# A fourth staging tile, an earlier place for one input tile and a later copy of turned keys in a one-core hybrid layer

## The chip, the core and the metric

The kernel runs on one core of a Trainium2 chip. The metric is the time of one execution on the device in microseconds (us), and the median of three runs is compared. TensorE (PE in the profile) multiplies matrices, VectorE (DVE), ScalarE (ACT) and GpSimd (POOL) work on elements, and SyncE (SP) issues nearly all transfers between device memory and on-chip memory. Each engine takes its instructions in the order in which the program lists them, so an instruction that waits holds up everything listed behind it on the same engine.

## The reference

One layer of a streaming encoder is computed for 2048 new rows (the prompt) and for 64 rows that continue an older stream (the sample), each row with 1024 features:

```
h = h + concat[ attnA(xn) * silu(gA), hgrn2(xn) * silu(gB) ] @ W_out,   xn = RMSNorm(h)
[aq, ak, av, ag, hq, hf, hi, hg] = split(xn @ W_in)        # eight groups of 512 columns
attnA: 8 heads x 64, chunks of 64 rows, each sees itself and the 8 chunks before it, plus a learned bias
hgrn2: 4 heads x 128, f = lb + (1-lb) sigmoid(hf), S_t = diag(f_t) S_{t-1} + (1-f_t) i_t^T, o_t = S_t^T q_t
y = RMSNorm(h)
```

Besides y, the new keys and values and the recurrent states are returned. Products are made in single precision's reduced form with operands split into a high and a low part, so each projection runs three passes (high by high, low by high, high by low).

## The kernel before

**Tiles and stages.** The rows are worked off in four super-blocks (`SUPER`): 512 rows, 512 rows and the 64 sample rows, 512, 512. In each there are 32 jobs: one job projects all rows of the super-block on 128 columns of W_in (24 matmuls for each piece of up to 512 rows, `project`, line 539). The jobs go by heads of the recurrence (`hf`, `hq`, `hi`, `hg`) and pairs of attention heads (`pg`, `pq`, `pk`, `pv`). A job's product lies in one of two PSUM banks named `acc`. It is taken out of there by an evacuation (`ev_q`, `ev_k`, `ev_v`, `ev_i` and others). These four kinds put it into a staging tile named `vT` of 128 x 512 numbers, of which there are three (`VTB`, line 31). `ev_v` and `ev_i` turn the tile by 32 x 32 blocks on VectorE and then send it through device memory and back (`turn_rows`, line 697: four transfers `way<-vT`, one transfer `vT<-way`), and the tile stays taken until the values are copied out. When the jobs are done, the output stage multiplies with W_out (by seven products for every 256 rows), adds the residual rows and normalizes.

**What sets the order.** The program is a planner that lists instructions for all engines by hand. `Plan` (line 52) holds a clock `now`, which goes on with each matmul listed, and for each other engine the time when it will be free by estimated costs (`act`, `dve`, `pool`, `dma`: a transfer is priced at 2.8 ns for each KB on SP plus 3500 ns). The main program lists the projections. Beside it run threads: evacuations, attention, recurrence, loads. A thread says what it waits for: a time, an engine's queue that will be at most 800 ns behind (`("D", t)`), a condition, or a token (`Tok`) that stands for a buffer. `pump` goes through the threads by rank, lower numbers first, and lists what is ready. Evacuations have rank 0, attention and recurrence 1, weights 2. The real chip then runs these fixed lists. Real waits come from semaphores, so where the estimate was too short an engine stands still.

**Input tiles.** `x_tile` (line 351) brings in 128 rows of the input (64 for the sample): it takes one of three `xn` buffers, loads it (line 358), squares it on ScalarE (line 368), makes 1/rms (lines 336 and 337), scales it on VectorE (line 382), waits until the older super-block has no more use of that half of `xh` and `xl` (line 387), and transposes it on TensorE by way of PSUM (line 397). `x_split` (line 404) copies the high part (409) and subtracts it for the low part (415). Only when the last transposes of a tile are listed is its `xn` buffer given back (line 401). The five tiles of super-block 1 are spawned together eight jobs before the end of super-block 0 (line 2104): rows 0 and 128 with rank 0.5, rows 256, 384 and 512 (the last is the sample's tile) with rank 0.6. The second half of super-block 1 needs the tiles 256, 384 and 512.

**Turned keys.** In super-blocks after the first the recurrence of the heads 0 and 1 turns its keys `kh` in the same way through device memory (line 1497, tiles `bl` and `way`). Line 1531 waits in the plan until the estimated time `rows["t"]` of the return. Then ScalarE copies the turned keys (line 1534) and TensorE multiplies them with the values (line 1560). The PSUM bank `g` and the token `rec` are held meanwhile.

**Output stage.** `residual` (line 1672) gives a residual tile one of four rooms. The fourth, named by the token `x5`, consists of a tile `rest` and a tile `sga`. `rest` and the token come in `out_rows_g` (line 2145). `out_load` takes two `vT` tiles for the inputs of every second 256 rows and a third for a sum.

Of the kernel before, what the change touches and what calls it, by code (L numbers as in the profile page):

```python
# [8 lines left out]
F32 = mybir.dt.float32  # L9
# [8 lines left out]
P = 128  # L18
# [9 lines left out]
RAWB = 2  # L28
XNB = 3
PRB = 4  # L30
VTB = 3
BIG = 1e30
NEVER = 1e30
QUEUE = 800.0
# [149 lines left out]
def hymba_step(  # L184
# [34 lines left out]
    wk = ctx.enter_context(tc.tile_pool(name="wk", bufs=2))  # L219
# [3 lines left out]
    C = Plan()  # L223
    uid = [0]

    def T(pool_, shape, dt, tag, **kw):
        uid[0] += 1
        return pool_.tile(list(shape), dt, tag=tag, name=f"{tag}_{uid[0]}", **kw)
# [122 lines left out]
    def x_tile(sb, half, c, here=None, gain=None):  # L351

        off, bn = SUPER[sb][3][half]
        rows = min(P, off + bn - c)
        if here is None:
            yield from tk["xn"].get()
            xn = T(px, [P, D], F32, "xn", bufs=XNB)
            sp.dma_start(xn[:rows], x_rows(sb, c, rows))
            t = C.dma(512)
        else:  # L360
            xn, t = here
        if half and not sb:
            yield lambda: x_there.get((0, 0, 0), (0, 0))[0] == 4
        yield "A", t
        yield from tk["ck"].get()
        junk = T(wk, [P, D], mybir.dt.bfloat16, "ck", bufs=1)
        ss = T(wk, [P, 1], F32, "ss", bufs=4)
        act.activation(junk[:rows], xn[:rows], AF.Square, accum_out=ss[:rows])
        r = rstd_of(ss, rows, D)
        tk["ck"].put()  # L370
        t = C.act(1700, t)
        have.add(f"r{c // P}")
        if not sb:
            yield lambda: "gain" in have and (not half or x_there.get((0, 0, 1), (0, 0))[0] == 4)
        g = g_in[:rows]
        cut = (slice(0, 512), slice(512, D)) if not sb else (slice(0, D),)
        ends = []
        for k0 in (0, 4):
            if k0 == 0 or not sb:
                c_ = cut[k0 // 4]  # L380
                yield "D", t
                dve.scalar_tensor_tensor(xn[:rows, c_], xn[:rows, c_], r[:rows], gain[k0 // 4] if gain else g[:, c_],
                                         ALU.mult, ALU.mult)
                t = C.dve(c_.stop - c_.start + 20, t)
                if k0:
                    have.add(f"s{c // P}")
            yield lambda: x_left.get((sb - 1, half), False)
            yield t
            tags = ("g", "tr") if sb else ("tr", "pv", "g") if half else ("tr", "pv", "acc")
            while not any(tk[x].n for x in tags):  # L390
                some = [tk[x].when() for x in tags]
                yield min(some) if min(some) < NEVER else C.now + 150.0
            tag = [x for x in tags if tk[x].n][0]
            tk[tag].take()
            pt = psum(tag, bufs={"g": 1, "pv": 1}.get(tag, 2))
            for kt in range(k0, k0 + 4):
                transpose(pt[:, (kt - k0) * P : (kt - k0) * P + rows], xn[:rows, kt * P : (kt + 1) * P],
                          ident[:rows, :rows])
            ends.append((k0, tag, pt, C.pe()))
            if k0 and here is None:  # L400
                tk["xn"].put(1, C.pe())
            C.spawn(x_split(sb, half, c, rows, *ends[-1]), 0 if sb or half else -1)
# [970 lines left out]
    def rec_block(r, off, bn, lastb):  # L1373
# [154 lines left out]
        if by_dma:  # L1528
            yield ta + 200.0
            yield lambda: "t" in rows  # L1530
            yield rows["t"]
            kn = tmp("k1").rearrange("p (c t) -> p c t", t=P)
            if nprc:
                act.copy(kn[:, :nprc].rearrange("p c (a j) -> p c a j", j=32),
                         kh[:, :full].rearrange("p (a c j) -> p c a j", a=4, j=32))
            if bn > full:
                act.copy(kn[:DEC, nprc], kh[:DEC, full : full + P])
                pool.memset(kn[DEC:, nprc], 0.0)
            t = C.act(bn, rows["t"])
            yield t + 200.0  # L1540
        else:
            yield max(ta, tkh) + 200.0
            tg = bank()
            for i, (cc, nbk, smp) in enumerate(chunks):
                w = nbk * 32
                transpose(tg[:w, i], kh[:, cc : cc + w], ident)
            t = C.pe()
            yield "A", t
            kn = tmp("k1").rearrange("p (c t) -> p c t", t=P)
            for cs, w in merged():  # L1550
                act.copy(kn[:w, cs], tg[:w, cs])
                if w < P:
                    pool.memset(kn[w:, cs], 0.0)
            t = C.act(bn, t)
            yield t + 200.0
# [110 lines left out]
    more = []  # L1666
# [352 lines left out]
    def program():  # L2019
# [66 lines left out]
        for sb in range(nsb):  # L2086
            last = sb == nsb - 1
            halves = SUPER[sb][3]
            blocks = SUPER[sb][2]
            if sb == 2:  # L2090
                C.spawn(out_weights(), 3)
            made = {}
            for u, (kind, g) in enumerate(JOBS[sb]):
                if u == len(JOBS[sb]) - 8:
                    if last:
                        C.spawn(out_load(0), 1.5)
                        C.spawn(out_load(1), 1.6)
                        for rows in (out_rows_w(), out_rows_g(), out_rows_x(), out_rows_a()):
                            C.spawn(rows, 2)
                    else:  # L2100
                        for half in range(2):
                            off, bn = SUPER[sb + 1][3][half]
                            for c in range(off, off + bn, P):
                                C.spawn(x_tile(sb + 1, half, c), 0.5 + 0.1 * half)
                if (kind[0], g) not in made:
                    d, evs = made[kind[0], g] = (head_jobs if kind[0] == "h" else pair_jobs)(sb, g)
                    C.spawn((recurrence if kind[0] == "h" else attention)(d), 1)
                evac = made[kind[0], g][1][kind[1]]

                if u == 1 or (u == len(JOBS[sb]) - 1 and not last):  # L2110
                    for half in range(2):
                        yield from project(j - 1, [halves[half]], before, half == 1,
                                           lambda part, k0: x_ready(sb, half, part, k0))
                        yield from project(j, [halves[half]], evac, half == 1,
                                           lambda part, k0: x_ready(sb, half, part, k0))
                        if u > 1:
                            x_left[sb, half] = True
                elif u != 0 and (last or u != len(JOBS[sb]) - 2):
                    yield from project(j, blocks, evac)
                    if u == len(JOBS[sb]) - 1:  # L2120
                        x_left[sb, 0] = x_left[sb, 1] = True
                before = evac
                j += 1
# [3 lines left out]
    def wo_load(k, w):  # L2127

        for part in range(2):
            hi = w(part, None)  # L2130
            for r, c in hi:
                sp.dma_start(f32(r), wod[k][:, part, c])
        wo[k] = (lambda part, kt: w(part, kt), C.dma(2048))

    def flat4(hi, lo):
        def w(part, kt):
            x = (hi, lo)[part]
            if kt is None:
                return [(x.rearrange("p (k n) -> p k n", k=4), slice(0, 4))]
            return x[:, kt * 512 : kt * 512 + 512]  # L2140

        return w


    def out_rows_g():
        yield lambda: done_g.get((len(SUPER) - 1, 3), 0) >= WIN
        yield C.now + 5000.0
        stkG.close()
        pw = ctx.enter_context(tc.tile_pool(name="pw", bufs=1, side="right"))
        turns = [0]  # L2150

        def slot():


            turns[0] += 1
            if turns[0] % 5 == 0:
                c = slice(8 * 512, 9 * 512)
                return [x.rearrange("p k n -> p (k n)")[:, c].rearrange("p (k t) -> p k t", t=P) for x in (xh, xl)]
            m = T(pw, [P, 2, 4, P], F32R, "slot", bufs=4)
            return m[:, 0], m[:, 1]  # L2160

        more.append(lambda: T(pw, [P, 512], F32, "rest"))
        tk["x5"].put()
        C.spawn(out_parts(slot), 1)
        wo_load(0, flat4(*(T(pw, [P, 4 * 512], F32R, f"b11{x}") for x in "hl")))

    def out_rows_w():
        yield lambda: len(order) - 1 in w_at
# [103 lines left out]
```

## Time and profile before

| what | value |
|---|---|
| median of three runs | 1229.98 us |
| lowest and highest run | 1228.17 and 1233.73 us |
| the profiled execution | 1236.85 us |
| its span, first to last instruction | 1234.9 us |
| TensorE busy | 1213.7 us, 98% of the span |
| VectorE, ScalarE, GpSimd busy | 897.7, 678.9, 416.2 us |
| mean granted TensorE clock | 0.995 |
| moved by DMA | 294.42 MB, 238 GB/s over the span |

A row of a timeline has start, duration, engine and line, operation, output<-input, shape and count, and in brackets the idle time of that engine just before and who ended it. A row of the waits has the total idle time in us, how often, and the longest. A row of the windows gives for a stretch of time its length, the busy time and number of instructions of PE, PEld (weight loads), DVE, ACT and POOL, then the granted TensorE clock as a share of the full clock, the DMA share and GB/s.

### The profile page before, as it was taken

Reading aid. Unit: us, or ns where it says so; the run is one execution under the profiler, and the core shown is the slowest. Engines: PE = TensorE matmul, PEld = TensorE weight load, DVE = VectorE, ACT = ScalarE, POOL = GpSimd, SP = SyncE. Lnnn points to the kernel's source line nnn. Section 1 sums busy time; section 2 is a strip of 40 time slices with the busy share of each in tenths; the row PEclk is TensorE's granted clock in tenths of the full one; section 3 lists DMA queues with packets and bytes.
Section 4 is the critical chain, followed back from the end, with each engine's and each line's share of the span. In section 5 each row is a group of like instructions: output and inputs, shape, how many; then the busy total and the mean of one; then the engine's idle time right before and its main releaser. Section 6 shows DMA issues by size and latency. Waiting matters only on the chain.

```text
span 1234.9 us, 22287 instructions
## 1 busy us (share of the span) xinstructions
PE 1213.7 (98%) x7914; PEld 1069.1 (87%) x7914; DVE 897.7 (73%) x1897; ACT 678.9 (55%) x1526; POOL 416.2 (34%) x715
## 2 busy tenths in 40 slices
PE   9999999899999999999999999999989999999997
PEld 8888888899999999998888888988778888888786
DVE  6697879766867687686587768775747665967775
ACT  6354546655565557574556566665636545644443
POOL 7665564111120110200232241133332203575543
PEclk9999999999999999999999999999989999999999
DMA  8898888657475585565887788587968586987431
GB/s 340 305 325 291 292 299 326 210 167 246 158 231 157 153 273 182 192 210 177 290 267 230 274 294 285 195 277 243 282 214 263 187 289 210 356 275 239 131 134 68
DMA packets 158328, 294.42 MB, mean 238 GB/s; under 512 B 51657, under 2 KB 98377, under 8 KB 140554
## 3 DMA queue, kind: packets, MB, share of 16 engines
q1 hardware_dynamic: 157784, 292.74, 71.0%
q8 instruction: 62, 1.02, 0.3%
q14 instruction: 48, 0.39, 0.1%
q10 hardware_dynamic: 434, 0.27, 0.1%
HBM read 198.52 MB, written 95.49 MB: 238 GB/s over the span
## 4 chain that ended last, share of the span: by engine, by line
PE 85%; DMA 9%; ACT 2%; DVE 1%; SPq 1%; issue 1%; POOL 0%; ACTq 0%; POOLq 0%; DVEq 0%
PE acc L249 56%; PE pv L249 7%; PE g L249 7%; PE tr L253 5%; PE s L249 5%; PE tr L249 4%; DMA vT<-way 1%; DMA bl<-way 1%; PE g L1369 1%; DMA w<-wd 1%; DMA ck<-in_cache_attn_v_dram 1%; DMA way<-vT 1%; DMA mixd<-ob 1%; DMA bias<-biasd 1%; DMA carry<-kd 1%
## 5 line engine op out<-in xcount | busy, mean ns | idle before, releaser
L249 PE MATMUL acc<-xh,w 128*128 128x512 f32 (+2 forms) x2720 | 563.5, 347 | 0.5 <-ACT vT L816 0.5
L249 PEld LDWEIGHTS acc<-xh,w 128*128 128x128 f32 x2720 | 437.1, 190 | 50.8 <-ACT vT L816 0.8
L249 PE MATMUL acc<-xl,w 128*128 128x512 f32 (+2 forms) x1360 | 293.8, 348 | 0.0
L249 PEld LDWEIGHTS acc<-xl,w 128*128 128x128 f32 x1360 | 223.3, 191 | 25.6
L967 ACT ACTIVATE pr<-pr,nm 128x640 f32<-128x640 f32 (+4 forms) x132 | 100.4, 761 | 61.2 <-DVE nm L950 60.2
L950 DVE CUSTOM_DVE_ANT_0 pr<-s,bias 128x640 f32<-128x640 f32 (+4 forms) x128 | 94.2, 736 | 48.2 <-PE s L249 45.6
L979 ACT CAST ph<-tr 128x512 fp32r<-128x512 f32 (+3 forms) x176 | 87.1, 507 | 75.3 <-PE tr L253 36.4
L982 DVE TENSOR_TENSOR ph<-tr,ph 128x512 fp32r<-128x512 f32 (+3 forms) x176 | 101.2, 589 | 28.3 <-ACT ph L979 27.3
L473 POOL TENSOR_TENSOR w<-wraw,w 128x256 fp32r<-128x256 f32 x120 | 101.6, 875 | 58.2 <-DVE w L468 33.4
L249 PE MATMUL pv<-ph,v 128*128 128x256 f32 (+2 forms) x344 | 97.1, 370 | 2.2 <-DVE ph L982 1.6
L253 PE MATMUL tr<-ident,pr 128*128 128x128 f32 x580 | 87.3, 273 | 0.9 <-DVE ph L982 0.9
L510 POOL TENSOR_TENSOR xn<-wraw,xn 128x256 fp32r<-128x256 f32 x48 | 39.8, 831 | 143.5 <-ACT xn L507 142.1
L1021 DVE TENSOR_TENSOR mixa<-mixa,pv 64x256 f32<-64x256 f32 (+1 forms) x144 | 56.8, 394 | 38.9 <-ACT mixa L1017 35.4
L1611 POOL TENSOR_TENSOR k<-ob 128x512 f32<-128x512 f32 (+2 forms) x20 | 18.4, 920 | 192.8 <-ACT ob L1602 192.5
L971 DVE TENSOR_SCALAR pr<-pr,sm 128x640 f32<-128x640 f32 (+4 forms) x132 | 79.8, 604 | 4.7
L253 PEld LDWEIGHTS tr<-ident,pr 128*128 128x128 f32 x580 | 69.7, 140 | 10.0 <-DVE ph L982 1.3
L1123 POOL TENSOR_TENSOR mixa<-mixa,sga 128x256 f32<-128x256 f32 (+1 forms) x36 | 28.7, 797 | 140.6 <-DVE mixa L1021 87.0
L249 PEld LDWEIGHTS pv<-ph,v 128*128 128x128 f32 x344 | 59.2, 190 | 10.4 <-issue 1.4
L575 ACT ACTIVATE sig<-acc 128x512 f32<-128x512 f32 (+2 forms) x63 | 31.9, 507 | 64.1 <-PE acc L249 63.0
L1017 ACT COPY mixa<-pv 64x256 f32<-64x256 f32 (+1 forms) x72 | 25.1, 349 | 60.3 <-PE pv L249 54.2
L249 PE MATMUL s<-kd,q 128*128 128x320 f32 (+2 forms) x232 | 55.8, 311 | 0.7 <-DVE nm L950 0.5
L249 PE MATMUL s<-kd,ql 128*128 128x320 f32 (+2 forms) x232 | 55.7, 310 | 0.0
(420 smaller groups left out, 2090.2 us busy)
## 6 DMA issues: line engine op xcount, KB each, us to landing
w<-wd SPq DMA_DIRECT2D x96, 1024.0 KB, 6.1
wd<-w SPq DMA_DIRECT2D x32, 1024.0 KB, 7.7
wraw<-in_w_in_dram SPq DMA_DIRECT2D x30, 512.0 KB, 5.5
wod<-xn SPq DMA_DIRECT2D x28, 512.0 KB, 5.3
xn<-in_x_prompt_dram SPq DMA_DIRECT2D x23, 512.0 KB, 5.3
bias<-biasd SPq DMA_DIRECT2D x24, 320.0 KB, 6.1
carry<-kd SPq DMA_DIRECT2D x12, 512.0 KB, 6.1
carry<-v SPq DMA_DIRECT2D x12, 512.0 KB, 7.2
```

The source lines that it names most:

```text
L249: pe.matmul(out, w, x, **kw)
L253: pe.transpose(out, x, idn)
L473: pool.tensor_sub(w[:, 1, k : k + 2], raw[:, k : k + 2], f32(w[:, 0, k : k + 2]))
L510: pool.tensor_sub(f32r(st[:, c.start + 512 : c.stop + 512]), src[:, c], st[:, c])
L575: act.activation(sig[:, :bn], acc, AF.Exp, scale=-1.0)
L950: dve.tensor_tensor_reduce(s[:, :nk].rearrange("p (a c) -> p a c", a=ns), sps[:, :ns, :kn], d.bias[:, h, bcol : bcol + nk].rearrange("p (a ...
L967: act.activation(s[:, :nk], s[:, :nk], AF.Exp, bias=nm[:, 0:1], scale=-1.0, accum_out=sm)
L971: dve.tensor_scalar(s[:, :nk], s[:, :nk], sm, None, ALU.mult)
L979: act.copy(ph[:krows, 0, :wid], pt[:krows, :wid])
L982: dve.tensor_sub(ph[:krows, 1, :wid], pt[:krows, :wid], f32(ph[:krows, 0, :wid]))
L1021: dve.tensor_add(mix[hs, :qn], mix[hs, :qn], pv[hs, i, :qn])
L1123: pool.tensor_mul(mix[:, :n], mix[:, :n], d.sg[:, g0 : g0 + n])
```

## The change

There are four edits. There are four `vT` tiles and four tokens for them, not three. A load of an input tile is priced by its rows, which for the sample's tile halves the size from 512 to 256. At the super-block's end an input tile of fewer than 128 rows, which is the sample's, is spawned with rank -0.5, ahead of the evacuations' rank 0. In the last super-block the copy of the turned keys is listed 3000 ns later in the plan. In the output stage the tile `rest` goes: the fourth room's first tile is one of the four `vT` tiles, it is taken after all projections of the last super-block are evacuated ("projected"), and only then is the token `x5` given.

```diff
-VTB = 3
+VTB = 4
@@ x_tile
             sp.dma_start(xn[:rows], x_rows(sb, c, rows))
-            t = C.dma(512)
+            t = C.dma(512 * rows / P)
@@ rec_block, if by_dma:
             yield lambda: "t" in rows
-            yield rows["t"]
+            yield rows["t"] + (3000.0 if sb == len(SUPER) - 1 else 0.0)
             kn = tmp("k1").rearrange("p (c t) -> p c t", t=P)
@@ program
                             for c in range(off, off + bn, P):
-                                C.spawn(x_tile(sb + 1, half, c), 0.5 + 0.1 * half)
+                                C.spawn(x_tile(sb + 1, half, c), 0.5 + 0.1 * half if off + bn - c >= P else -0.5)
@@ out_rows_g
-        more.append(lambda: T(pw, [P, 512], F32, "rest"))
-        tk["x5"].put()
         C.spawn(out_parts(slot), 1)
         wo_load(0, flat4(*(T(pw, [P, 4 * 512], F32R, f"b11{x}") for x in "hl")))
+        yield lambda: "projected" in have
+        yield from tk["vT"].get()
+        more.append(lambda: T(wk, [P, 512], F32, "vT", bufs=VTB))
+        tk["x5"].put()
```

## The prediction

> **What bounds the kernel now.** I read the page first, then whom TensorE waits for, then windows and timelines around its two longest waits.
>
> ```profile
> span 1234.9 us, 22287 instructions
> PE 1213.7 (98%) x7914; PEld 1069.1 (87%) x7914; DVE 897.7 (73%) x1897; ACT 678.9 (55%) x1526; POOL 416.2 (34%) x715
> ```
>
> TensorE is busy for 1213.7 of 1234.9 us. No edit takes a matmul away, so only its 21.2 us of idle time can be gained, and what it loses at a lower clock. Its waits:
>
> ```profile
> PE g L249 <- ACT k L1534: 3.8, 2, 3.4
> PE g L253 <- DVE xn L382: 3.3, 1, 3.3
> PE tr L253 <- DVE ph L982: 1.7, 2, 0.9
> PE pv L249 <- DVE ph L982: 1.6, 2, 1.0
> PE pv L2068 <- POOL one L279: 1.4, 1, 1.4
> PE g L249 <- DVE So L1572: 0.7, 2, 0.4
> PE pv L249 <- DVE v L683: 0.6, 1, 0.6
> PE s L249 <- DVE nm L950: 0.5, 1, 0.5
> PE acc L249 <- ACT vT L816: 0.5, 1, 0.5
> ```
>
> Two waits stand out, and two edits aim at them: the turned keys (line 1534) and an input tile (line 382). Without the one at the start (line 2068), the short ones and the 0.4 us left of the first row sum to 6.0 us. There is hardly a sign that staging tiles are short: TensorE waited for an evacuation into `vT` once, for 0.5 us.
>
> Windows around the two waits, and one with two short gaps, show a second cost in the clock column (after the busy times):
>
> ```profile
> 240.00:244.00 4.00, 0.70 (x8) 0.58 (x8) 3.65 (x8) 2.28 (x7) 0.00 (x0) 1.00 0.86 320
> 245.00:249.00 4.00, 4.00 (x18) 3.80 (x17) 3.93 (x17) 3.04 (x12) 2.02 (x9) 0.57 0.17 62
> 904.00:908.00 4.00, 0.97 (x5) 0.46 (x3) 0.00 (x0) 0.29 (x1) 0.00 (x0) 0.95 0.97 347
> 908.00:915.00 7.00, 6.62 (x22) 5.69 (x23) 4.73 (x11) 2.88 (x7) 3.09 (x4) 0.54 0.50 143
> 789.00:796.00 7.00, 5.71 (x44) 5.00 (x43) 6.80 (x14) 5.54 (x13) 1.99 (x2) 1.00 0.76 231
> ```
>
> After each long wait TensorE goes on at about half the clock: 4.00 us at 0.57 lose 4.00 x 0.43 = 1.72 us, 6.62 us at 0.54 lose 6.62 x 0.46 = 3.05 us. The last stretch, with 1.29 us of gaps, stays at 1.00. So the input tile's wait costs 3.30 + 1.72 = 5.02 us, the keys' 3.41 + 3.05 = 6.46 us (hundredths from the timelines below), together 11.48 us.
>
> By the Trainium skill (TensorE: Matmul & The Clock Gate, Part 1), the clock falls to half after an idle window of about 3.4 us and returns after a busy one, the windows running freely: 1.7 us for each wait. The trace agrees at the first (1.72) and has nearly twice that at the second. By the rule's figure in place of 3.05 the forecast below would be 1225.7 us.
>
> **The turned keys, 3000 ns later.** Where the second wait comes from:
>
> ```profile
> 889.58 2.01 PE L249 MATMUL acc<-xl,w 128*128 128x512 f32 x8
> 897.80 1.00 SPq L715 DMA_DIRECT2D bl<-way  x1
> 907.71 0.62 ACT L1534 COPY k<-bl 128x512 f32<-128x512 f32 x1 [6.74 <-DMA bl<-way]
> 908.24 0.36 ACT L979 CAST ph<-tr 128x256 fp32r<-128x256 f32 x1
> 908.38 2.08 PE L249 MATMUL g<-gi,k 128*128 128x128 f32 x8 [3.41 <-ACT k L1534]
> 912.39 2.50 PE L249 MATMUL acc<-xl,w 128*128 128x512 f32 x6
> DMA to landing us min/median/max: 1.4/2.5/9.9
> ```
>
> The way back was issued at 897.80 and landed 9.9 us later, where the median of tile `bl`'s transfers is 2.5. The copy held ScalarE for 6.74 us, and behind it in ScalarE's list stood the copy for `ph` (908.24) and more, on which later matmuls depend. The edit lists the copy, and the matmuls on the keys with it, 3.0 us of planned time later, so that other matmuls pass them. There are such: between 910.0 and 914.7 stand ten of a running projection (the row at 912.39 has six) and two on `ph`, twelve at 2.01 / 8 = 0.25 us at full clock, or 3.0 us, and ScalarE lists the copy for `ph` before the wait then. The wait of 3.41 shrinks to 0.41 us, a gap of the sort after which the clock stayed at 1.00. Gain: 3.0 + 3.05 = 6.05 us. The bounds: 6.46 if the way back is faster in the new order, nothing if it is 3 us slower still. I take 6.05, since the edit leaves the transfer and its neighbours where they are.
>
> Behind the copy on its path are the state updates on VectorE, the store of a state on SP, two more rounds on TensorE, GpSimd's square (line 1611) and the store to `mixd`; all move by the same 3 us, and the bank `g` and `rec` are held as long. The next recurrence has room for that:
>
> ```profile
> 924.03 0.75 DVE L1629 SCALAR_TENSOR_TENSOR ob<-ob,gnorm,k 128x512 f32<-128x512 f32 x1
> 943.61 0.68 DVE L1388 TENSOR_TENSOR bm<-gb 128x512 f32<-128x512 f32 x1
> ```
>
> One ends its norm at 924.8, the next begins at 943.6, so 19 us cover 3; without them the 3 us would be paid in full. Cost taken: nothing.
>
> **The sample's input tile ahead of evacuations.** Here the plan's tokens decide, more than the rank that the edit names:
>
> ```profile
> 174.95 1.40 SPq L358 DMA_DIRECT2D xn<-in_x_prompt_dram  x3
> 225.46 0.33 SPq L358 DMA_DIRECT2D xn<-in_x_prompt_dram  x1
> 227.97 0.57 SPq L358 DMA_DIRECT2D xn<-in_x_sample_dram  x1
> 232.69 1.04 PE L253 MATMUL tr<-ident,xn 128*128 128x128 f32 x8
> 234.29 1.06 ACT L368 ACTIVATE ck<-xn 64x1024 bf16<-64x1024 f32 x1
> 235.80 0.20 ACT L337 ACTIVATE rstd<-rstd 64x1 f32<-64x1 f32 x1
> 238.85 0.29 DVE L683 TENSOR_TENSOR v<-vT,v 128x128 fp32r<-128x128 f32 x1 [0.27 <-ACT v L680]
> 240.00 0.57 ACT L409 CAST xh<-tr 128x512 fp32r<-128x512 f32 x1
> 242.42 1.27 DVE L382 SCALAR_TENSOR_TENSOR xn<-xn,rstd,gin 64x1024 f32<-64x1024 f32 x1
> 243.83 0.43 PE L253 MATMUL g<-ident,xn 64*128 64x64 f32 x4 [3.30 <-DVE xn L382]
> 244.30 0.37 ACT L409 CAST xh<-g 128x256 fp32r<-128x256 f32 x1 [1.95 <-PE g L253]
> ```
>
> Three tiles (rows 0, 128, 256) are loaded near 175, into all three buffers. Tile 384 and the sample's come when the first two give theirs back, at 225.46 and 227.97. The last one's 1/rms was there at 236.00, but VectorE scaled it at 242.42, behind evacuations from 238.85 on, and TensorE, out of other work, waited from 240.53.
>
> With rank -0.5 the sample's thread is first in `pump` also when the tokens are given out. So it takes one of the three buffers near 175, and its load, square, 1/rms and scaling move from 228 to 244 down to 175 to 191, where tile 256 stood. But it can't be transposed there: its half of `xh` is free only at about 232.69, where the edited plan puts it and the old one tile 256. Until then it keeps its buffer, so tile 256 is loaded at about 225.5 and tile 384 at about 228. Tile 384 has rank 0.6 as the sample's tile had. It gets the last place with the same wait behind the evacuations, and with more to do: each of its two high copies takes 0.57 rather than 0.37 us. SP's queue has 512 KB in that place and 256 KB in the earlier one; the transfers behind it are the bias windows and a weight, due later. The price of 256 shortens the plan's SP clock by 0.72 us at 175, where nothing waits.
>
> So the 5.02 us stay and about 2 x 0.20 = 0.4 us are added. The bounds: -5.02 if the tile comes forward after all (VectorE's list from 238.85 to 242.42 is 3.57 us, more than the 3.30), and some +1.5 if the doubled load holds ScalarE. I take +0.4, since the queue that made the wait is unchanged and only the tile in it differs.
>
> **The fourth tile.** It adds no instruction. It lets the plan list an evacuation earlier, so every list after the first shortage is in another order. What the trace shows to be gained is 0.5 us at `acc`; what it can cost is rivals two and three. I take nothing. In the output stage a fourth `vT` tile replaces `rest`:
>
> ```profile
> L1701 SPq DMA_DIRECT2D rest<-in_x_prompt_dram x2: 430/920/1411, 1099.8 to 1137.1; - x2
> ```
>
> That room is first used at 1099.8, and it needs the last scores as it did before, which come after the projections. The later token costs nothing, and the loads are as many.
>
> **The sum.** 6.05 - 0.4 = 5.65 us. The profiled execution took 1236.85 us (1.95 over its span), so 1231.2. It lies above all three runs; the median is 1229.98 / 1236.85 = 0.99445 of it, which makes **1224.4 us**. Its own range is 1221 to 1227. About 0.5% (6.1 us, the line being at 1223.8) is what a measurement of this kernel can tell from no change, and the forecast lies at that line.
>
> **The rivals.**
>
> *One, both long waits go.* The sample's tile still comes last or the new order clears VectorE's list near 240, and no tile is late. For: 3.57 us of evacuations stood before the scaling. Against: the buffers. Gain 5.02 + 6.05 = 11.07, so 1219 us. With the 6.0 us of short waits closed too, 1213.
>
> *Two, a new long wait opens elsewhere.* The two of now cost 5.02 and 6.46, on the mean 5.7. One more eats the gain: 1230 us. For: all lists change, and ScalarE has many places where it waits in line for a round trip:
>
> ```profile
> ACT v L680 <- DMA vT<-way: 16.9, 9, 5.0
> ACT gi L1308 <- DMA vT<-way: 12.0, 10, 3.8
> ```
>
> Against: these 19 waits, of up to 5.0 us, stopped TensorE for no more than 1 us now.
>
> *Three, slower: the round trips crowd.* With four tiles, four trips can be open at once rather than three. If transfers then land later than the plan allows, ScalarE's waits above outlast TensorE's listed work, each time for idle time and half a clock. It decides from the third: 3 x 5.7 - 5.65 = 11.5 us lost, or 1241 us. Against: the number of trips is the same.
>
> *Four, the clock stays down.* The keys' wait shrinks, but the gaps left around it keep the clock low: only 3.0 of the 6.05 are gained, 1227.4 us. The row from 789 to 796 speaks against it. The Trainium skill (TensorE: Matmul & The Clock Gate, "A second HAM failure mode: psum-queue depth-cycling") tells of short idles between matmul groups making the clock go to and fro; in that row the trace disagrees.
>
> *Five, the keys are as late in their new place.* Nothing is gained: 1230.4 us.
>
> **How the numbers follow.** The forecast has 0.36, rival one 0.24 (0.04 of it with the short waits closed), two 0.18, three 0.13, four 0.04, five 0.05. Half of the forecast lies beyond 0.5%: faster 0.18 + 0.24 = 0.42, slower 0.13 and a little of rival two, 0.15, the rest 0.43. The range goes from 1215, between the two ends of rival one, to 1233, which is rival two with the 1.5 us of tile 384 and rounding; it leaves out rival three and the 0.04.
>
> **What would show it.** Right: TensorE's row for line 1534 has under 0.5 us as its longest, and the clock after it is 1.00; a row for line 382 still has 3 to 4 us, now on a tile of 128 rows, with the sample's load near 175 and a prompt load near 228. Wrong: no row for line 382, or new rows of 3 us and more, above all behind `vT<-way`; a busy time of TensorE that differs by more than the clock explains.

## The result and the profile after

| | before | changed |
|---|---|---|
| median of seven runs | 1229.98 us | 1225.01 us |
| ratio, with its 95% interval | | 0.9948 (0.993 to 0.9966) |
| profiled execution | 1236.85 us | 1225.67 us |
| its span | 1234.9 us | 1223.9 us |

One of the seven runs before took 1491.62 us in a slow state of the chip, and the ratios here and below leave such runs out. The changed kernel is 5.0 us faster, 0.5%, close to the 1224.4 us predicted. But the two profiled executions differ by 11.2 us, more than twice as much. That gap is the first thing to explain.

The page's head after:

```profile
span 1223.9 us, 22269 instructions
PE 1209.3 (99%) x7914; PEld 1064.9 (87%) x7914; DVE 895.2 (73%) x1897; ACT 681.1 (56%) x1526; POOL 413.8 (34%) x715
```

TensorE's instructions are as many as before. Its idle time (span less busy time) fell from 21.2 to 14.6 us, its busy time by 4.4 us. The waits of TensorE after (total, times, longest):

```profile
PE acc L249 <- ACT vT L795: 1.6, 1, 1.6
PE pv L2068 <- POOL one L279: 1.4, 1, 1.4
PE g L249 <- ACT k L1534: 1.2, 1, 1.2
PE g L249 <- DVE So L1572: 1.1, 2, 0.8
PE pv L249 <- DVE ph L982: 1.0, 1, 1.0
PE acc L249 <- ACT xh L409: 0.6, 1, 0.6
```

Both long waits are gone, also the one that was to stay: there is no row for line 382. (The row for line 1534 lies at 388, in super-block 1.) The windows at the two places, and the timeline there:

```profile
241.00:245.00 4.00, 3.23 (x22) 2.36 (x21) 3.65 (x13) 3.90 (x13) 0.00 (x0) 1.00 0.87 312
245.00:250.00 5.00, 5.00 (x34) 5.00 (x35) 4.93 (x15) 4.61 (x14) 1.58 (x6) 1.00 0.15 37
900.00:905.00 5.00, 5.00 (x28) 4.28 (x27) 2.37 (x5) 1.76 (x5) 2.77 (x4) 1.00 0.92 338
```

```profile
175.82 0.57 SPq L358 DMA_DIRECT2D xn<-in_x_sample_dram  x1
176.48 1.01 SPq L358 DMA_DIRECT2D xn<-in_x_prompt_dram  x2
226.75 0.35 SPq L358 DMA_DIRECT2D xn<-in_x_prompt_dram  x1
231.15 0.38 SPq L358 DMA_DIRECT2D xn<-in_x_prompt_dram  x1
233.27 0.71 PE L253 MATMUL tr<-ident,xn 64*128 64x64 f32 x8
240.16 0.20 ACT L337 ACTIVATE rstd<-rstd 128x1 f32<-128x1 f32 x1
240.39 1.28 DVE L382 SCALAR_TENSOR_TENSOR xn<-xn,rstd,gin 128x1024 f32<-128x1024 f32 x1
241.91 0.60 PE L253 MATMUL g<-ident,xn 128*128 128x128 f32 x4
```

The clock is 1.00 in all three windows. The sample's tile did take a buffer near 175, and tile 384 did get the last place (load at 231.15, scaled at 240.39). But its scaling follows right on its 1/rms (240.36), and TensorE comes to its transposes 0.24 us after the scaling ended.

### The profile page after: what moved, and what is told of

Read it like the earlier page. It is cut to its first block, busy times and chain, and to the rows that moved or that the text cites. A ratio compares the mean times of both kernels' runs of the same rounds, so it can differ in the third digit from the quotient of the medians.

```text
span 1223.9 us, 22269 instructions
## 1 busy us (share of the span) xinstructions
PE 1209.3 (99%) x7914; PEld 1064.9 (87%) x7914; DVE 895.2 (73%) x1897; ACT 681.1 (56%) x1526; POOL 413.8 (34%) x715
## 4 chain that ended last, share of the span: by engine, by line
PE 90%; DMA 5%; DVE 2%; ACT 1%; SPq 1%; issue 1%; POOL 0%; DVEq 0%; ACTq 0%; POOLq 0%
PE acc L249 59%; PE pv L249 7%; PE g L249 7%; PE tr L253 6%; PE s L249 5%; PE tr L249 4%; PE g L1369 1%; DMA vT<-way 1%; DMA ck<-in_cache_attn_v_dram 1%; DMA So<-in_state_hgrn_dram 1%; PE g L253 1%; DMA carry<-kd 1%; DMA way<-sig 1%; DMA bias<-biasd 0%; DMA lbg<-in_lb_gamma_dram 0%
## 5 line engine op out<-in xcount | busy, mean ns | idle before, releaser
L249 PEld LDWEIGHTS acc<-xl,w 128*128 128x128 f32 x1360 | 220.1, 189 | 25.0
```

The source lines that it names most:

```text
L249: pe.matmul(out, w, x, **kw)
```

## The experiments

Each kernel was timed in up to twelve runs beside the unchanged kernel on the same chip. The first four went together, then the next four, then the last four. Each kernel is the one before with the edit shown, if nothing else is said.

### The unchanged kernel again

> The unchanged kernel once more, with another profile. Theory A: the profiled execution of before (1236.85 us) had longer waits and more time at half the clock than its usual run, which is why the two profiles differ by 11.2 us and the medians by 5.0. Then this profile shows a total near 1230, with the waits for line 382 or line 1534 shorter or less time at half the clock, and the ratio is 1.000 +- 0.003. Theory B: the waits are as long in every execution and the changed kernel loses some 6 us elsewhere. Then this profile shows both waits again at 3.0 us or more, each with a stretch at half the clock, and a span within 2 us of 1234.9.

Median 1230.48 us, ratio 1.000 (0.9985 to 1.0014); the profiled execution took 1233.98 us. Its waits of TensorE:

```profile
PE g L249 <- ACT k L1534: 3.7, 1, 3.7
PE g L253 <- DVE xn L382: 3.3, 1, 3.3
```

The windows behind them:

```profile
244.00:249.00 5.00, 5.00 (x23) 4.88 (x24) 4.48 (x19) 3.85 (x14) 1.77 (x9) 0.50 0.15 56
906.00:913.00 7.00, 6.80 (x25) 5.91 (x26) 4.92 (x11) 2.70 (x7) 3.27 (x5) 0.59 0.44 131
```

Both waits are there again, each with half a clock behind it, as theory B has it, though the span of 1232.1 us misses its bound by 0.8 us. The median is 3.5 us lower than this profiled execution, as theory A has it. So neither stands alone: what one profile shows is real, and dearer than the usual run. The mean granted clock, which is recorded for every run, agrees on the whole. Of the 34 other runs of this kernel beside these four, the two at 0.993 took 1234.7 us on the mean, the three at 0.995 took 1232.3, the eighteen at 0.997 took 1229.3 and the six at 0.998 took 1230.1. The two profiled executions stood at 0.995 and 0.993. By the clock that their traces record, TensorE ran at half the clock behind the two waits for 3.41 + 6.83 = 10.24 us in the profile of before and for 2 x 6.83 = 13.66 us in this one. In the profiled executions of all kernels here that stood at 0.997 or above, the stretches behind waits sum to 6.83 us at most.

### The fourth tile alone

```diff
-VTB = 3
+VTB = 4
@@ out_rows_g: the tile rest replaced by a vT tile, as in the change
```

> Only the fourth staging tile with the room in the output stage that goes with it. The theory of the prediction: it takes nothing out of any path, ratio 1.000 +- 0.003, and the waits for lines 382 and 1534 remain in its profile. Rival: the fourth tile clears VectorE's list near 240 us and is what took the input tile's wait away; then no wait for line 382 over 1 us, and a ratio of 0.996 to 0.998.

Ratio 1.0006 (0.9991 to 1.0021): no gain, as the theory had it. But the two old waits are gone, and another took their place:

```profile
PE pv L249 <- DVE ph L982: 4.9, 1, 4.9
```

```profile
1009.35 0.62 ACT L1308 COPY gi<-vT 128x512 f32<-128x512 f32 x1 [8.40 <-DMA vT<-way]
```

It ends at 1012 us, behind ScalarE's copy of the recurrence's values (line 1308), which the next run shows more closely. The sample's tile has its old place in this kernel (loaded at 228.07), and yet its wait is gone: VectorE's redrawn list scales it at 236.97, not 242.42.

### The sample's tile alone

```diff
-            t = C.dma(512)
+            t = C.dma(512 * rows / P)
-                                C.spawn(x_tile(sb + 1, half, c), 0.5 + 0.1 * half)
+                                C.spawn(x_tile(sb + 1, half, c), 0.5 + 0.1 * half if off + bn - c >= P else -0.5)
```

> Only the sample's input tile ahead of the evacuations, with its price by rows. The theory of the prediction: the wait passes to the tile of rows 384, so a wait of 3 to 4 us for line 382 stays, on a tile of 128 rows, and the ratio is 1.000 +- 0.003. Rival: this edit alone takes the wait away, so no wait for line 382 over 1 us and a ratio of 0.996 to 0.998; the wait for line 1534 may stay.

Ratio 1.0007 (0.9994 to 1.002). The theory is refuted in its mechanism, the rival in its number: there is no wait for line 382, the longest near 240 is 0.6 us, and yet nothing is gained. The waits and the timeline show what took it back, at 1010:

```profile
PE pv L249 <- DVE ph L982: 4.4, 1, 4.4
```

```profile
1003.15 0.34 SPq L715 DMA_DIRECT2D vT<-way  x1
1009.52 0.62 ACT L1308 COPY gi<-vT 128x512 f32<-128x512 f32 x1 [7.89 <-DMA vT<-way]
1010.04 0.82 ACT L967 ACTIVATE pr<-pr,nm 128x640 f32<-128x640 f32 x1
1012.22 0.48 PE L249 MATMUL pv<-ph,v 128*128 128x256 f32 x2 [4.43 <-DVE ph L982]
```

ScalarE stood 7.89 us at the copy of the recurrence's values (line 1308), whose way back through device memory was issued at 1003.15 and landed 6.4 us later. Listed behind it were a softmax and a copy for `ph`, and TensorE waited 4.43 us for those. This is rival two, a new long wait behind `vT<-way`. It is not the crowding of rival three, as this kernel has three staging tiles.

The keys' wait at 900 is gone in these lists too, without the later copy:

```profile
894.47 0.62 ACT L1534 COPY k<-bl 128x512 f32<-128x512 f32 x1 [0.91 <-DMA bl<-way]
```

The way back was issued at 891.18 and took 3.3 us, and TensorE did not wait (its 1.0 us for line 1534 lie at 387, in super-block 1).

### The later copy alone

```diff
-            yield rows["t"]
+            yield rows["t"] + (3000.0 if sb == len(SUPER) - 1 else 0.0)
```

> Only the later copy of the turned keys in the last super-block. The order of the lists differs from before only from about 900 us on. The theory of the prediction: the wait for line 1534 shrinks to under 0.5 us, the clock stays at 1.00 after it, the wait for line 382 stays; ratio 0.995 if the keys' wait is as costly in every run as in the profile of before (6.05 us), 0.997 to 0.999 if that profile was an unlucky one. Rival: the keys' wait moves along with the copy, ratio 1.000.

Ratio 1.0009 (0.9997 to 1.0021): nothing gained, although the profile shows the keys' wait gone in the last super-block, as the theory had it (the 0.4 us left for line 1534 lie at 306, in super-block 1; the wait for line 382 is still there with 3.1 us).

### The keys not waited for

```diff
-                         kh[:, :full].rearrange("p (a c j) -> p c a j", a=4, j=32))
+                         (eb if sb == len(SUPER) - 1 and h == 1 else kh)[:, :full].rearrange("p (a c j) -> p c a j", a=4, j=32))
```

> The kernel before with the same instruction lists on every engine; only the copy of the turned keys of head 1 in the last super-block reads a tile that is long there, not the turned keys (so that head's last state and output are not the reference's). The way through device memory runs as before, but nobody waits for it. If the keys' wait costs in every run what the profile of before shows, ratio 0.9948 (6.46 us). If it is a wait of the profiled executions only, which the run of the later copy alone suggests (1.0009), ratio 0.999 to 1.001. Its idle time alone, with the clock mostly kept, would give 0.997.

Ratio 0.9979 (0.9967 to 0.9991). In a usual run the keys' wait costs 0.0021 x 1230 = 2.6 us (1.1 to 4.1 by the interval), not the 6.46 of the profile of before.

### The input tile not waited for

```diff
-                dve.scalar_tensor_tensor(xn[:rows, c_], xn[:rows, c_], r[:rows], gain[k0 // 4] if gain else g[:, c_],
+                dve.scalar_tensor_tensor(xn[rows : 2 * rows, c_] if rows < P else xn[:rows, c_], xn[:rows, c_], r[:rows], gain[k0 // 4] if gain else g[:, c_],
```

> The kernel before with the same instruction lists on every engine; only the scaling of the sample's input tile writes into rows of its buffer that nobody reads, so that TensorE transposes the unscaled rows without a wait for VectorE (the sample's outputs are not the reference's). If the input tile's wait is what the changed kernel gained, ratio 0.996 (5.0 us), no wait for line 382. If the next thing late behind it takes its place (the tile's copies for xh and xl), a wait for lines 409 or 415 of 2 to 3 us and a ratio of 0.998 to 1.000.

Ratio 0.9999 (0.9983 to 1.0015). The waits of TensorE, and the place:

```profile
PE s L249 <- DVE nm L950: 3.3, 1, 3.3
```

```profile
240.68 0.46 PE L253 MATMUL g<-ident,xn 64*128 64x64 f32 x4
244.72 0.58 PE L249 MATMUL s<-kd,q 128*128 128x256 f32 x1 [3.33 <-DVE nm L950]
```

Something else took the place, though not the copies expected: the transposes ran at once, and TensorE then waited the same 3.3 us for line 950, a reduction of scores, which stands behind the scaling in VectorE's list. So the tile's wait was not what cost the time. VectorE's list was 3.3 us behind TensorE's there, 1.3 of it the scaling itself, and with these lists taking one wait away only uncovers the next.

The same lists gave a third look at the keys' round trip. In the profiles of before, of its repetition and of this kernel:

```profile
897.80 1.00 SPq L715 DMA_DIRECT2D bl<-way  x1
...
907.71 0.62 ACT L1534 COPY k<-bl 128x512 f32<-128x512 f32 x1 [6.74 <-DMA bl<-way]
```

```profile
895.88 0.55 SPq L715 DMA_DIRECT2D bl<-way  x1
905.53 0.62 ACT L1534 COPY k<-bl 128x512 f32<-128x512 f32 x1 [7.04 <-DMA bl<-way]
```

```profile
895.30 0.33 SPq L715 DMA_DIRECT2D bl<-way  x1
902.74 0.62 ACT L1534 COPY k<-bl 128x512 f32<-128x512 f32 x1 [4.05 <-DMA bl<-way]
903.41 1.16 PE L249 MATMUL g<-gi,k 128*128 128x128 f32 x8 [0.72 <-ACT k L1534]
```

The way back took 9.9, 9.6 and 7.4 us, and TensorE waited 3.41, 3.74 and 0.72 us. The wait differs from one execution to the next, so a single profile can't tell what an edit did to it.

### Neither waited for

Both edits at once.

> Both of these at once, lists unchanged. The sum of the two if they are independent: 0.991 if both cost what the profile of before shows (11.5 us), 0.996 if the keys' wait costs nothing in a usual run.

Ratio 0.9981 (0.9968 to 0.9995). Neither sum that was expected came (0.991 or 0.996): it is like the keys alone, since the tile's wait is replaced by the one for line 950 (3.3 us again).

### The change without the fourth tile

The kernel after, with `VTB = 3` and the tile `rest` as before.

> The changed kernel without the fourth staging tile: the sample's tile ahead, its price and the later copy, with three tiles and the tile rest as before. TensorE's list is then the same as that of the changed kernel. So the theory that the fourth tile gains nothing expects the whole gain: 0.9948 +- 0.002, and in the profile no wait over 2 us. Rival: the fourth buffer keeps transfers apart that now wait for each other; ratio 0.997 to 1.000.

Ratio 0.9942 (0.9925 to 0.9958), median 1224.31 us: the whole gain. TensorE's list is the same as in the changed kernel. The fourth tile and its room can be left away. One wait was over the 2 us expected: 2.2 us for line 1534 in super-block 1.

### The sample's tile alone, its trip at 1010 not waited for

On the kernel with the sample's tile alone:

```diff
-                             it[:rows, c : c + w].rearrange("p (a t j) -> p a t j", a=4, j=32))
+                             (reset if sb == len(SUPER) - 1 and h == 3 else it)[:rows, c : c + w].rearrange("p (a t j) -> p a t j", a=4, j=32))
```

> The kernel with only the sample's tile ahead (ratio 1.0007), its lists unchanged on every engine, but ScalarE's copy of the recurrence's values for head 3 in the last super-block (line 1308) reads a constant tile instead of the staging tile that comes back from device memory, so nobody waits for that trip (that head's output and last state are not the reference's). Theory: the sample's edit does win the 5 to 6 us near 240 us, and this one copy, which held ScalarE for 7.9 us and TensorE for 4.4 us at 1010, gives them back; then 0.994 to 0.996, as the whole change. Rival: the sample's edit wins nothing in usual runs and the gain comes from the lists after 900 us; then 0.998 to 1.000.

Ratio 0.9968 (0.9956 to 0.9981), no wait over 1.5 us. Against 1.0007 with the wait, this one copy had cost 0.0039 x 1230 = 4.8 us. So the sample's edit does win, and a late trip in the redrawn lists takes it back. The number lies between those of the theory and the rival, and falls short of the whole change by 0.002 to 0.0026. Nor is it shown that the place near 240 is what wins: the keys' wait, worth 2.6 us, is gone in these lists too, which leaves 0.0032 x 1230 - 2.6 = 1.3 us, less than the intervals can tell from nothing.

### 1500 and 6000 ns in place of 3000

On the change without the fourth tile.

> The sample's tile ahead and the copy of the turned keys 1500 ns later, not 3000, three staging tiles. Theory: with the sample's edit the keys are not waited for in any case, and what the number does is to draw another order of the lists from 900 us on, with waits of its own at other places: anything from 0.994 (no long wait) to 1.001 (one long wait). Rival: the keys need the delay; then it lies halfway, 0.997, with a wait of 1 to 2 us for line 1534 near 900.

> The same with 6000 ns. Theory: again another order from 900 us on, 0.994 to 1.001, no wait for line 1534 in the last super-block. Rival: a longer delay is only safer and as good as 3000: 0.994 to 0.995.

The ratios are 0.9979 (0.9966 to 0.9991) and 0.9977 (0.9963 to 0.9992). With 0 ns it was 1.0007, with 3000 ns 0.9942. The gain does not rise or fall along with the delay, and with neither number does ScalarE or TensorE wait for the keys in the last super-block. The delay redraws the lists from 900 us on; 3000 ns drew the best of these four, though the interval of the whole change (up to 0.9966) just reaches those of 1500 and 6000 ns. ScalarE's waits at line 1308, with 1500 and 6000 ns:

```profile
1007.29 0.62 ACT L1308 COPY gi<-vT 128x512 f32<-128x512 f32 x1 [5.00 <-DMA vT<-way]
```

```profile
1008.93 0.62 ACT L1308 COPY gi<-vT 128x512 f32<-128x512 f32 x1 [4.18 <-DMA vT<-way]
```

Behind them TensorE waits 1.5 and 1.0 us for line 982. In the whole change ScalarE's wait is 3.51 us, and TensorE does not wait. This is less than the 4 us or so by which these kernels are slower, and the rest is not shown: the profile with 6000 ns has no wait of TensorE over 1.6 us, and no stretch at half the clock behind one.

### The rank alone

```diff
-                                C.spawn(x_tile(sb + 1, half, c), 0.5 + 0.1 * half)
+                                C.spawn(x_tile(sb + 1, half, c), 0.5 + 0.1 * half if off + bn - c >= P else -0.5)
```

> Only the rank -0.5 of the sample's tile, without its price by rows; no later copy, three staging tiles. Theory: the tile that gets a buffer first frees VectorE's list near 240 us, so no wait of 2 us or more for lines 382 or 950 there; as the lists after 900 us keep nearly the order of before, the keys' wait stays there and no wait at 1010 is drawn; 0.996 to 0.998. Rival, the prediction's: the last place passes to the tile of rows 384 and the wait near 240 stays at 3 us or more; 0.999 to 1.001.

Ratio 0.9976 (0.9962 to 0.999). Near 240:

```profile
PE g L253 <- DVE xn L382: 2.5, 1, 2.5
```

```profile
230.37 0.38 SPq L358 DMA_DIRECT2D xn<-in_x_prompt_dram  x1
241.68 1.28 DVE L382 SCALAR_TENSOR_TENSOR xn<-xn,rstd,gin 128x1024 f32<-128x1024 f32 x1
243.11 1.09 PE L253 MATMUL g<-ident,xn 128*128 128x128 f32 x4 [2.52 <-DVE xn L382]
```

This is the picture that the prediction drew for the rank: a prompt tile of 128 rows in the last place, behind evacuations on VectorE, and TensorE waiting, for 2.5 us. The keys' wait was 1.3 us in this execution, which lies between those that one and the same list showed above. So the rank alone does not free VectorE's list; with the price by rows it does. The theory of this run had the number right and the mechanism wrong, the rival nearly the reverse: the kernel gains without taking the wait away. Why it gains is not shown.

No run is faster than the changed kernel by more than the intervals. The change without the fourth tile is as fast as the whole and simpler.

## Why the prediction was right or wrong

The number was right: 1224.4 against 1225.0 us. That it came out so near is luck. It is the sum of two steps that were wrong in opposite directions, and the prediction's own sign of being wrong, no row for line 382, came.

**Where the time could go** was right. No matmul went away, and the gain is idle time and time at half the clock: in the profiled executions 6.6 us less idle, 4.4 us less busy. The trace of before has 10.24 us at half the clock behind its two waits, of which 0.77 us lie in a wait; the rest loses (10.24 - 0.77) x 0.5 = 4.7 us. The trace of the changed kernel has none behind its waits.

**The input tile** failed, at the sentence that the price by rows shortens the plan's SP clock "by 0.72 us at 175, where nothing waits". The tokens did what was said, and with the rank alone the wait passed to tile 384. But nothing has to wait for the 0.72 us to matter: the plan lists by its clock, and with rank and price together TensorE's list differs from before from 184.9 us on (with the rank alone from 194.7). In that order VectorE had tile 384 scaled before TensorE came for it. Also wrong was to price "the tile's wait" as the tile's. The run with the unscaled rows shows VectorE's list as the thing that was late, with the next wait as long as the one taken away, and the fourth tile alone made the wait go without touching the tile's place.

**Rank against evacuations** is not the point in the changed kernel: with 0.4 in place of -0.5, behind the evacuations and ahead of the other tiles, the planner lists the very same instructions on all engines. Without the price by rows, the two ranks give different lists.

**The keys** were right in direction and too dear: 6.05 us by the profile, 2.6 in a usual run. The prediction scaled the profiled execution's sum with 1229.98 / 1236.85, as if all parts of it were longer by the same share. But the wait itself differs between executions of one list (3.74 to 0.72 us), and so does the time at half the clock behind it, so the profile's price for this one place was too high by more than that share. The later copy did take the wait away when it stood alone, as foretold, and yet won nothing (1.0009), so the redrawn lists behind 900 us give its 2.6 us back. Where, is only partly shown: its profile has waits of 1.4 and 1.5 us for line 982 after 1000. In the changed kernel it isn't the delay that was needed for the keys, as the sample's edit alone had their wait gone. What the delay did there was to draw lists without the long wait at 1010.

**The fourth tile** was right at nothing for the whole (0.9942 without it). Alone it redrew everything from 233 us on and exchanged two long waits for one of 4.9 us.

**Rival one**, both waits gone, is what happened in the profile. Its 1219 us carried the same mis-scaling. **Rival two** happened in the parts: the fourth tile alone and the sample's tile alone each opened one long wait, both at the same round trip, on which ScalarE stood in line. Rival three's crowding by a fourth tile is not seen: one of these two kernels has three tiles, and the whole change is as fast with four.

What the sample's edit is worth by itself in a usual run stays open: every way to take it alone also redraws the lists after it. Open too is why the keys' way back took 9.9 us in one execution and 7.4 in another of the same lists, and 3.3 us in other lists.

## What to carry to other kernels

Where a planner lists all engines by an estimated clock, any edit of a price or a rank draws a new order from there to the end: judge an edit by whole runs of several such orders, and look for the list that is late, not for the instruction at which the wait shows. Before a wait is priced, look at it in two or three profiled executions, and compare their total with the median: here an execution above all three timed runs showed waits and slow stretches that the usual run doesn't have in full. To learn what a wait is worth, let the waiting instruction read something that is long there, with all lists unchanged: here the answer was 2.6 of 6.46 us for one wait and nothing for the other, where the next wait took its place.

## What the runs showed of the hardware

The clock fell after waits far shorter than the two of before. In the kernel with 1500 ns, TensorE waited once for 1.86 us near 387, and the windows behind that are:

```profile
386.00:388.00 2.00, 0.32 (x2) 0.32 (x3) 0.21 (x1) 0.64 (x2) 0.00 (x0) 1.00 0.59 174
388.00:390.00 2.00, 2.00 (x15) 2.00 (x14) 1.21 (x5) 1.61 (x6) 0.00 (x0) 0.78 0.18 55
390.00:392.00 2.00, 2.00 (x8) 1.61 (x7) 2.00 (x5) 0.92 (x4) 0.00 (x0) 0.50 0.60 111
392.00:394.00 2.00, 2.00 (x15) 1.99 (x14) 0.93 (x4) 1.48 (x4) 0.00 (x0) 0.86 0.98 414
```

The last three lose 2.00 x (0.22 + 0.50 + 0.14) = 1.72 us, as much as behind the 3.30 us of before. In the kernel with the sample's tile alone, 4.43 us of waiting cost no more: 1.78 x 0.29 + 2.00 x 0.50 + 2.00 x 0.06 = 1.64 us:

```profile
1012.00:1014.00 2.00, 1.78 (x10) 1.71 (x11) 1.29 (x3) 1.97 (x4) 0.00 (x0) 0.71 0.88 132
1014.00:1016.00 2.00, 2.00 (x9) 1.90 (x8) 1.10 (x4) 1.59 (x4) 0.00 (x0) 0.50 0.81 340
1016.00:1018.00 2.00, 2.00 (x13) 1.78 (x12) 1.53 (x5) 0.92 (x2) 0.00 (x0) 0.94 0.28 119
```

In the fourteen traces of this case, each of the 13 waits of 1.86 us or more has a stretch at half the clock in its end or right behind it, and none of the shorter ones has, the longest being 1.76 us (in the change without the fourth tile, ended at 289.5). Each stretch lasts 3.41 us (seven of them) or 6.83 us (six), so that it costs up to 1.7 or 3.4 us, and the wait's length doesn't say which: the wait near 240 us, with the same lists, was 3.30 us long with 3.41 us at half the clock in the profile of before, and 3.33 us long with 6.83 us in its repetition. This is what parts the prediction's 1.72 and 3.05 us.

The Trainium skill (TensorE: Matmul & The Clock Gate, Part 1) asks for an idle window of about 3.4 us before the clock falls. An estimate from that figure, half the pulses of one window, is 1.7 us for each fall, which fits the shorter stretches. The length of the wait doesn't fit: 1.86 us of it were enough here, with 0.18 us idle in the 6 us before.
